# Two transformer blocks on one core: where the normalized activations h lie in SBUF, from the second norm on

## The chip, the core and the metric

The kernel runs on one core of a Trainium2 chip. The metric is the device time of one execution in microseconds (us); nanoseconds (ns) are used for single instructions. Lower is better. The kernel before took 881.18 us (median of three runs, 878.16 to 882.48). The engines are called as the profile calls them: PE is TensorE's matmul, PEld its weight load, DVE is VectorE, ACT is ScalarE, POOL is GpSimd and SP is SyncE, whose queue issues the loads.

## The reference, cut to what matters

256 tokens of width 1024 pass two blocks of a network; another 256 context tokens enter the first block's mixer. All data is float32. In short:

```python
# block 1
h   = modulate(rmsnorm(x), shift1, scale1)            # first norm; the same for the context
x  += gate1 * hgrn2_mixer(h_ctx, h, w_in[1024, 5120], w_out)
h   = modulate(rmsnorm(x), shift2, scale2)            # second norm
x  += gate2 * (silu(conv(h @ Wg)) * conv(h @ Wv)) @ w_down     # d_ff = 2816
x   = rmsnorm(x)
# block 2
h   = rmsnorm(x)                                       # third norm
p   = h @ w_in_2                                       # retention and window attention, gates
x  += rmsnorm((sig(ga) * (ret @ w_ro) + sig(gs) * (swa @ w_so)) @ w_o2)
h   = rmsnorm(x)                                       # fourth norm
x  += rmsnorm(relu(h @ w_up_2)**2 @ w_down_2)          # d_ff = 4096
```

Nearly all of the arithmetic is in the products with weights of 1024 or more rows.

## The kernel before, in words

**Three matmuls for one.** A float32 operand is split into a rounded part and a rest, both in the type fp32r. A product is then three matmuls: rounded times rounded, rounded times rest, rest times rounded. For weights, ACT writes the rounded part (tile `hi`, line 155) from the loaded tile `raw`, and DVE writes the rest (tile `lo`, line 156). For the normalized activations the two parts are `hTh` and `hTl` (lines 357 and 358): 128 partitions, 8 blocks of 1024 features over 128 partitions, 512 columns. In the first block's mixer the columns are 256 context tokens and 256 tokens; from the second norm on columns 0 to 255 are the tokens, and columns 256 to 511 hold the output of the retention later.

**Two ways to multiply with h.** A matmul has a stationary operand, 128 columns that a weight load (LDWEIGHTS) puts into the array, and a moving operand, 256 or 512 columns that stream through it. In the profile's form `out<-moving,stationary` they can be told apart.
- `fm_product` (lines 377 to 390) with `mm3` (lines 349 to 354): weights are stationary, h moves, 256 columns. One chunk of weights makes 2 x 8 x 3 = 48 matmuls. Rows `x<-hTh,hi`, `x<-hTl,hi`, `x<-hTh,lo` and the same with `m<-`.
- `mm3_rows` (lines 335 to 347), used right after a norm: h is stationary, 128 tokens at a time, and the weights move. Rows `x<-hi,hTh` and so on, 256 columns wide after the second and the fourth norm, 512 wide after the third. The mixer's `v_half` (line 756) does the same through `mm3`.

`row_product` (line 895) is the second product of each pair: activations (`ah`, `al`, or `yh`, `yl`) are stationary and weights move, 512 columns: rows `m<-hi,ah`. It reads no h.

**Order.** The program is written out in the order in which each engine executes it. PE works through: the modulation and the first two projections (to 60 us), the mixer's projections with the scan's small matmuls between (to 264 us), its output product, the second norm with the first three chunks of the up projection as `mm3_rows` (288 to 308 us), then the feed-forward part, in which two `fm_product` of 48 matmuls and one `row_product` of 24 alternate (to 475 us); the third norm with the v projection as `mm3_rows` (478 to 502 us), block 2's projections as `fm_product` with the attention's small matmuls put between them by `tick` (to 605 us), the gates and the two output products (to 686 us), the fourth norm with `mm3_rows` (688 to 702 us), and the last feed-forward part, in which one `fm_product` and one `row_product` alternate (to 869 us). Loads run on SP's queue, ahead of use, as buffers come free; `pump` (line 116) issues loads and splits.

**Where the tiles lie.** The pools are laid out one behind the other in the order of the code, and a tile has the same byte offset in all 128 partitions. In the built program of the kernel before:

```
raw buffers  18944 ..  (8 of 4096 bytes)          0 mod 512
oTs          51712                                0
hTh          59904   (16384 bytes)                0
hTl          76288   (16384 bytes)                0
x0, x1, vr   92672 ..                             0
main hi, lo  110016 ..  (5 + 5 of 4096 bytes)   448
later pools  behind them: the first stage's and the mixer's output's buffers 192,
             the buffers of all later stages (hi, lo, ah, al, swh, swl) 448
```

Every slice of h that a matmul reads starts at a multiple of 512 bytes from `hTh` or `hTl`, and every slice of weights at a multiple of 512 bytes from its buffer, so the place modulo 512 is that of the tile. In this text the **offset** of a matmul is the place of its moving operand less the place of the stationary operand that is loaded for the next matmul, modulo 512. In the kernel before it is 64 where h moves over weights at 448, and 448 (that is, 64 behind) where such weights move over h.

Of the kernel before, what the change touches and what calls it, by code (L numbers as in the profile page):

```python
# [10 lines left out]
F32R = mybir.dt.float32r  # L11
# [6 lines left out]
KT = 8  # L18
# [33 lines left out]
def kernel(ctx: ExitStack, tc: tile.TileContext, a, out):  # L52
# [5 lines left out]
    res = ctx.enter_context(tc.tile_pool(name="res", bufs=1))  # L58
# [4 lines left out]
    def bank(tag):  # L63
        return ps.tile([128, 512], F32, tag=tag, name=tag, bufs=4)
# [102 lines left out]
    def use(i, keep=None, ahead=None):  # L167

        assert i == at_["u"], (i, at_["u"])
        at_["u"] += 1  # L170
        at_["rel"] = chunks[i if keep is None else keep][0]
        a0, a1 = chunks[i]
        pump(len(halves) if ahead is None else a1 + ahead)
        assert at_["s"] >= a1
        w = []
        for j in range(a0, a1):
            r = ready.pop(j)
            for k in range(halves[j][1] if r else 0):
                w.append((r[0][:, k, :], None if r[1] is None else r[1][:, k, :]))
        return w  # L180
# [5 lines left out]
    def part_done(i):  # L186

        at_["rel"] = max(at_["rel"], chunks[i][0] + 1)
        pump(len(halves))
# [159 lines left out]
    def mm3(o, w, x, start, stop):  # L349
        wh, wl = w  # L350
        xh, xl = x
        t_.matmul(o, wh, xh, start=start, stop=False)  # L352
        t_.matmul(o, wh, xl, start=False, stop=False)  # L353
        t_.matmul(o, wl, xh, start=False, stop=stop)  # L354

    oTs = res.tile([128, 4, 512], F32, name="oTs")
    hTh = res.tile([128, KT, 512], F32R, name="hTh")
    hTl = res.tile([128, KT, 512], F32R, name="hTl")

    def hT(k, c0, c1):  # L360
        return hTh[:, k, c0:c1], hTl[:, k, c0:c1]
# [170 lines left out]
    for i in range(2):  # L532
        t = res.tile([128, D], F32, name=f"x{i}")
# [174 lines left out]
    for p in range(4):  # L708
# [9 lines left out]
        else:  # L718
            for d in range(2):
                i = C["ff" if d == 0 else "fb", p]  # L720
# [174 lines left out]
    def row_product(name, n, lhs, done):  # L895

        acc = []

        def mms(j, w, kk, tok, half):
            c = slice(half * 512, half * 512 + 512)
            mm3(acc[2 * tok + half], lhs(j, kk, tok), (w[kk][0][:, c], w[kk][1][:, c]),
                j == 0 and kk == 0, j == n - 1 and kk == 1)

        def go(j):
            if not acc:
                acc.extend(bank("m") for _ in range(4))
            w = use(C[name, j])
            for kk in range(2):  # L910
                for tok in range(2):
                    for half in range(2):
                        mms(j, w, kk, tok, half)
                if kk == 0:
                    part_done(C[name, j])

        def finish(*limits):
            tail = range(n - SKEW, n)
            w = {}
            for j in tail:  # L920
                w[j] = use(C[name, j], keep=C[name, n - SKEW])
                for kk in range(2):
                    for half in range(2):
                        mms(j, w[j], kk, 0, half)
            d0, d1 = done(0, acc[0:2]), done(1, acc[2:4])
            f0 = [next(d0) for _ in range(4)][-1]
            for j in tail:
                for kk in range(2):
                    mms(j, w[j], kk, 1, 0)
            next(d1)  # L930
            for j in tail:
                if f0 and j == n - 1:
                    f0()
                    pump(limits[0])
                for kk in range(2):
                    mms(j, w[j], kk, 1, 1)
                    at_["rel"] = chunks[C[name, j]][0] + kk + 1
            for limit in limits[1:]:
                pump(limit, True)
            for _ in limits[1:]:  # L940
                next(d1)
                if held:
                    held.pop(0)()
            while held:
                held.pop(0)()
            return [x for x in d1][-1]
        return go, finish
# [8 lines left out]
    def act_lhs(store):  # L956
        def f(j, kk, tok):
            h_, l_ = store[j]
            c = slice(kk * 256 + tok * 128, kk * 256 + tok * 128 + 128)
            return h_[:, c], l_[:, c]  # L960
        return f

    def to_hT(pool, n, tok, A, B=None, tag="hf"):


        c = slice(tok * 128, tok * 128 + 128)
        z, hf = [], []
        for kq in range(2):
            z.append(bank("x"))
            for i in range(4):  # L970
                k = 4 * kq + i
                t_.transpose(z[kq][:, i * 128:(i + 1) * 128], n[:, k * 128:(k + 1) * 128], ident)
            hf.append(pool.tile([128, 512], F32, tag=tag, name="hf", bufs=2).rearrange("p (k t) -> p k t", k=4))
        z0 = z[0].rearrange("p (k t) -> p k t", k=4)

        def per_k(v):
            return v[:, 0:4].rearrange("p (k o) -> p k o", o=1).to_broadcast([128, 4, 128])

        for i in range(4):
            k = 4 + i  # L980
            zi = z[1][:, i * 128:(i + 1) * 128]
            if B is None:
                s_.activation(hf[1][:, i, :], zi, AF.Identity, scale=A[:, k:k + 1])
            else:
                s_.activation(hf[1][:, i, :], zi, AF.Identity, scale=A[:, k:k + 1], bias=B[:, k:k + 1])
        s_.activation(hTh[:, 4:8, c], hf[1], AF.Copy)
        v_.tensor_tensor(hf[0], z0, per_k(A), op=OP.mult)
        if B is not None:
            v_.tensor_tensor(hf[0], hf[0], per_k(B), op=OP.add)
        v_.tensor_copy(hTh[:, 0:4, c], hf[0])  # L990
        for kq in range(2):
            o = slice(4 * kq, 4 * kq + 4)
            v_.tensor_tensor(hTl[:, o, c], hf[kq], hTh[:, o, c].bitcast(F32), op=OP.subtract)
# [11 lines left out]
    def o1_done(tok, acc):  # L1005
# [10 lines left out]
        scaled(y, x, r)  # L1016
        yield lambda: to_hT(ok, y, tok, AB2[:, 0, :], AB2[:, 1, :])

    go, finish = row_product("o1", 4, act_lhs(ys), o1_done)
    for p in range(4 - SKEW):  # L1020
        go(p)
# [144 lines left out]
    for tok in range(2):  # L1166
        for j in range(2):
# [5 lines left out]
            def done(k):  # L1173
                if tok and k % 2:
                    at_["rel"] = chunks[C["vr", j, 0]][0] + k // 2 + 1
                    pump(len(halves))
# [324 lines left out]
```

## Time and profile before

| | |
|---|---|
| runs before, median (lowest, highest) | 881.18 us (878.16, 882.48) |
| the profiled execution's own time | 877.26 us |
| its span, first to last instruction | 875.5 us |
| mean granted clock of PE | 0.997 |
| PE busy, share of the span | 859.9 us, 98% |
| PEld, DVE, ACT busy | 780.3, 599.5, 497.7 us |
| HBM read | 159.93 MB |

Matmuls overlap: the profile gives each a duration that includes its way through the array, 0.28 us for 256 columns, while the next one starts after about 0.12 us. The pace is therefore read from start to start, in the list in order of time: the difference of two start times over the number of matmuls between them. "Busy" alone does not show it.

### The profile page before, as it was taken

The page shows a single profiled execution, that of the slowest core. Times are in us where ns is not written, and L with a number is a line of the kernel's source. Part 1 is how long each engine was busy: PE and PEld are TensorE (multiplying, and loading weights), DVE is VectorE, ACT ScalarE, POOL GpSimd, SP SyncE. Part 2 cuts the span into 40 slices and gives each one's busy share as a digit, 9 for nine tenths or more (in the row PEclk, how much of TensorE's full clock was granted, in tenths as well). Part 3 has the DMA queues.
Part 4 walks back from the last instruction along what each step waited for, and adds up shares of the span by engine and source line. Part 5 has one row for each costly group of instructions (what it writes and reads, how often), then busy time and mean ns, then how long its engine had stood idle before and what let it go on. Part 6 is the DMA issues. An engine that isn't in the chain of part 4 may idle for free.

```text
span 875.5 us, 15429 instructions
## 1 busy us (share of the span) xinstructions
PE 859.9 (98%) x6216; PEld 780.3 (89%) x6216; DVE 599.5 (68%) x935; ACT 497.7 (57%) x807; POOL 16.3 (2%) x27
## 2 busy tenths in 40 slices
PE   8999999999999999999999999999999999999997
PEld 7688898989988999999997799999999899999995
DVE  5577969776878688877768646765495687555532
ACT  4587474855856667555555646666553665444421
POOL 0000000000000000000000000000000100000000
PEclk9999999999999999999999999999999999999999
DMA  9892654825437368776753573545786097655401
GB/s 352 274 346 101 181 181 128 281 74 173 141 122 256 107 219 275 259 235 215 261 171 73 181 206 107 157 130 155 205 302 205 3 314 247 189 188 187 150 1 49
DMA packets 116360, 161.99 MB, mean 185 GB/s; under 512 B 13888, under 2 KB 95808, under 8 KB 116288
## 3 DMA queue, kind: packets, MB, share of 16 engines
q1 hardware_dynamic: 113984, 155.80, 55.6%
q10 hardware_dynamic: 2304, 5.20, 1.7%
q8 instruction: 49, 0.80, 0.4%
q14 instruction: 23, 0.19, 0.1%
HBM read 159.93 MB, written 1.05 MB: 184 GB/s over the span
## 4 chain that ended last, share of the span: by engine, by line
PE 89%; DVE 5%; ACT 3%; DMA 1%; issue 1%; POOL 0%; SPq 0%; POOLq 0%; DVEq 0%; ACTq 0%
PE m L352 17%; PE m L354 17%; PE m L353 17%; PE x L352 8%; PE x L354 8%; PE x L353 8%; PE x L685 1%; DVE lo L156 1%; PE m L342 1%; PE x L342 1%; PE m L343 1%; PE m L338 1%; DMA raw<-in_f0w_dram 1%; PE x L343 1%; PE x L338 1%
## 5 line engine op out<-in xcount | busy, mean ns | idle before, releaser
L156 DVE TENSOR_TENSOR lo<-raw,hi 128x1024 fp32r<-128x1024 f32 (+1 forms) x248 | 291.0, 1203 | 130.7 <-ACT hi L155 130.6
L155 ACT ACTIVATE hi<-raw 128x1024 fp32r<-128x1024 f32 (+1 forms) x248 | 249.6, 1039 | 117.6 <-PE x L353 50.7
L352 PE MATMUL m<-hTh,hi 128*128 128x256 f32 (+1 forms) x560 | 178.8, 319 | 1.5 <-ACT hTh L422 1.5
L353 PE MATMUL m<-hTl,hi 128*128 128x256 f32 (+1 forms) x560 | 171.0, 305 | 0.5 <-DVE hTl L429 0.5
L354 PE MATMUL m<-hTh,lo 128*128 128x256 f32 (+1 forms) x560 | 171.3, 306 | 0.1
L352 PE MATMUL x<-hTh,hi 128*128 128x256 f32 x592 | 166.0, 280 | 0.0
L354 PE MATMUL x<-hTh,lo 128*128 128x256 f32 x592 | 164.9, 279 | 0.0
L353 PE MATMUL x<-hTl,hi 128*128 128x256 f32 x592 | 164.8, 278 | 0.0
L352 PEld LDWEIGHTS m<-hTh,hi 128*128 128x128 f32 x560 | 105.7, 189 | 12.3 <-issue 5.1
L352 PEld LDWEIGHTS x<-hTh,hi 128*128 128x128 f32 x592 | 111.1, 188 | 1.0 <-ACT hi L155 0.2
L353 PEld LDWEIGHTS x<-hTl,hi 128*128 128x128 f32 x592 | 110.8, 187 | 1.0 <-issue 0.2
L354 PEld LDWEIGHTS x<-hTh,lo 128*128 128x128 f32 x592 | 111.3, 188 | 0.0
L353 PEld LDWEIGHTS m<-hTl,hi 128*128 128x128 f32 x560 | 105.8, 189 | 6.0 <-DVE hTl L429 1.1
L354 PEld LDWEIGHTS m<-hTh,lo 128*128 128x128 f32 x560 | 105.3, 188 | 5.8 <-DVE lo L156 0.3
L352 PE MATMUL m<-hi,ah 128*128 128x512 f32 x248 | 97.3, 392 | 0.0
L354 PE MATMUL m<-hi,al 128*128 128x512 f32 x248 | 96.8, 390 | 0.0
L353 PE MATMUL m<-lo,ah 128*128 128x512 f32 x248 | 96.5, 389 | 0.0
L354 PEld LDWEIGHTS m<-hi,al 128*128 128x128 f32 x248 | 46.5, 188 | 10.6 <-DVE al L1142 0.4
L353 PEld LDWEIGHTS m<-lo,ah 128*128 128x128 f32 x248 | 46.6, 188 | 8.9
L352 PEld LDWEIGHTS m<-hi,ah 128*128 128x128 f32 x248 | 46.6, 188 | 8.9 <-ACT ah L1138 0.2
L576 DVE SCALAR_TENSOR_TENSOR vr<-raw,cs,vr 128x1024 f32<-128x1024 f32 x28 | 35.9, 1281 | 0.4
L352 PE MATMUL m<-hi,hTh 128*128 128x256 f32 x128 | 35.8, 280 | 0.0
(302 smaller groups left out, 1251.5 us busy)
## 6 DMA issues: line engine op xcount, KB each, us to landing
raw<-in_ffn_w_up_dram SPq DMA_DIRECT2D x44, 512.0 KB, 5.6
raw<-in_w_in_dram SPq DMA_DIRECT2D x42, 512.0 KB, 4.1
raw<-in_hg_w_in_dram SPq DMA_DIRECT2D x36, 512.0 KB, 5.3
raw<-in_w_ada_dram SPq DMA_DIRECT2D x32, 512.0 KB, 5.5
raw<-in_w_up_dram SPq DMA_DIRECT2D x32, 512.0 KB, 4.9
raw<-in_w_down_dram SPq DMA_DIRECT2D x32, 512.0 KB, 3.6
raw<-in_ffn_w_down_dram SPq DMA_DIRECT2D x22, 512.0 KB, 4.5
raw<-in_ada_dram SPq DMA_DIRECT2D x16, 512.0 KB, 6.5
```

What stands on the lines that cost most here:

```text
L155: s_.activation(h[:, :w], r[:, :w], AF.Copy)
L156: held.append(lambda r=r, h=h, l=l, w=w: v_.tensor_tensor(l[:, :w], r[:, :w], h[:, :w].bitcast(F32), op=OP.subtract))
L338: t_.matmul(o, hTl[:, k, c], w[k][0], start=False, stop=k == KT - 1)
L342: t_.matmul(o, hTh[:, k, c], w[k][0], start=k == 0, stop=False)
L343: t_.matmul(o, hTh[:, k, c], w[k][1], start=False, stop=False)
L352: t_.matmul(o, wh, xh, start=start, stop=False)
L353: t_.matmul(o, wh, xl, start=False, stop=False)
L354: t_.matmul(o, wl, xh, start=False, stop=stop)
L576: v_.scalar_tensor_tensor(acc, w[kk][0], cs[:, k:k + 1], acc, op0=OP.mult, op1=OP.add)
L685: t_.matmul(z[:, b * 128:(b + 1) * 128], l, r, start=i == 0, stop=i == len(terms) - 1)
```

## The change

One tile of 2 x 8 x 512 + 32 elements (32,896 bytes a partition) takes the place of `hTh` and `hTl`. Up to the mixer's end the two parts are views of it from element 32 on, that is from byte 128 on; from `hTh, hTl = h_at(0)` on, ahead of the mixer's output product, they are views from element 0 on. The functions that read or write h (`hT`, `mm3_rows`, `to_hT`, `re_t`) take the names from the enclosing function, so they follow. Everything that is allocated after h moves up by 128 bytes; what is allocated before it (`raw`, `oTs`, `ident`, `ones`, `vecs`) stays.

```diff
     oTs = res.tile([128, 4, 512], F32, name="oTs")
-    hTh = res.tile([128, KT, 512], F32R, name="hTh")
-    hTl = res.tile([128, KT, 512], F32R, name="hTl")
+
+
+    h_mem = res.tile([128, 2 * KT * 512 + 32], F32R, name="hT")
+
+    def h_at(o):
+        return [h_mem[:, i:i + KT * 512].rearrange("p (k t) -> p k t", k=KT) for i in (o, o + KT * 512)]
+
+    hTh, hTl = h_at(32)
 
     def hT(k, c0, c1):
         return hTh[:, k, c0:c1], hTl[:, k, c0:c1]
@@ -1016,6 +1022,7 @@
         scaled(y, x, r)
         yield lambda: to_hT(ok, y, tok, AB2[:, 0, :], AB2[:, 1, :])
 
+    hTh, hTl = h_at(0)
     go, finish = row_product("o1", 4, act_lhs(ys), o1_done)
```

## Rows read from the trace of the kernel before

**Rows 1.** The page's part 1: busy us, share of the span, instructions, by engine.
```profile
PE 859.9 (98%) x6216; PEld 780.3 (89%) x6216; DVE 599.5 (68%) x935; ACT 497.7 (57%) x807; POOL 16.3 (2%) x27
```
**Rows 2.** The page's part 4: the chain of work that ended last, by engine.
```profile
PE 89%; DVE 5%; ACT 3%; DMA 1%; issue 1%; POOL 0%; SPq 0%; POOLq 0%; DVEq 0%; ACTq 0%
```
**Rows 3.** Windows: stretch, length, busy us of PE, PEld, DVE, ACT, POOL, clock, DMA.
```profile
329.90:447.20 117.30, 117.30 (x841) 110.51 (x840) 95.68 (x132) 68.86 (x92) 0.00 (x0) 1.00 0.73 240
502.40:605.60 103.20, 103.20 (x847) 98.79 (x846) 62.04 (x118) 61.76 (x130) 2.79 (x4) 1.00 0.52 152
719.10:868.80 149.70, 149.70 (x936) 135.25 (x935) 77.94 (x81) 64.52 (x79) 0.54 (x1) 1.00 0.47 148
```
**Rows 4.** PE in order of time: start us, us; two feed-forward products from 329.91.
```profile
329.91 0.28 PE L352 MATMUL x<-hTh,hi 128*128 128x256 f32 x1
...
341.22 0.40 PE L352 MATMUL m<-hi,ah 128*128 128x512 f32 x1
```
**Rows 5.** PE in order of time, three feed-forward products behind transposes.
```profile
308.24 0.28 PE L353 MATMUL x<-hTl,hi 128*128 128x256 f32 x1
...
324.45 0.39 PE L352 MATMUL m<-hi,ah 128*128 128x512 f32 x1
```
**Rows 6.** Groups by line and form in windows 329.9 to 447.2 and 605.5 to 637.
```profile
L352 PE MATMUL x<-hTh,hi 128*128 128x256 f32 x224 | 62.7, 280 | 0.0
...
L352 PE MATMUL m<-hTh,hi 128*128 128x256 f32 x76 | 21.1, 277 | 0.0
```
**Rows 7.** PE in order of time, block 2's projections, and the last feed-forward product.
```profile
540.81 0.28 PE L353 MATMUL m<-hTl,hi 128*128 128x256 f32 x1
...
541.99 0.28 PE L354 MATMUL m<-hTh,lo 128*128 128x256 f32 x1
...
847.13 0.28 PE L354 MATMUL x<-hTh,lo 128*128 128x256 f32 x1
```
**Rows 8.** PE in order of time, the mixer's v_half: weights move, h is stationary.
```profile
60.13 0.29 PE L352 MATMUL m<-hi,hTh 128*128 128x256 f32 x1
60.25 0.28 PE L353 MATMUL m<-lo,hTh 128*128 128x256 f32 x1
60.37 0.28 PE L354 MATMUL m<-hi,hTl 128*128 128x256 f32 x1
60.48 0.28 PE L352 MATMUL m<-hi,hTh 128*128 128x256 f32 x1
...
71.02 0.39 PE L352 MATMUL m<-hTh,hi 128*128 128x512 f32 x1
```
**Rows 9.** PE in order of time, mm3_rows after the second and the fourth norm.
```profile
300.57 0.28 PE L342 MATMUL x<-hi,hTh 128*128 128x256 f32 x1
...
304.57 0.28 PE L342 MATMUL x<-hi,hTh 128*128 128x256 f32 x1
...
697.33 0.28 PE L342 MATMUL x<-hi,hTh 128*128 128x256 f32 x1
```
**Rows 10.** PE in order of time, swh over weights, both at 448.
```profile
637.09 0.28 PE L353 MATMUL x<-swl,hi 128*128 128x256 f32 x1
...
639.85 0.28 PE L352 MATMUL x<-hTh,hi 128*128 128x256 f32 x1
```
**Rows 11.** PE in order of time, 512 columns wide, three pairs of operands.
```profile
84.53 0.39 PE L354 MATMUL m<-hTh,lo 128*128 128x512 f32 x1
...
329.69 0.39 PE L354 MATMUL m<-hi,al 128*128 128x512 f32 x1
...
478.35 0.40 PE L342 MATMUL m<-hi,hTh 128*128 128x512 f32 x1
...
479.28 0.40 PE L338 MATMUL m<-hi,hTl 128*128 128x512 f32 x1
```
**Rows 12.** Groups by line in windows 265 to 300 and 329 to 447: DVE's split.
```profile
L156 DVE TENSOR_TENSOR lo<-raw,hi 128x1024 fp32r<-128x1024 f32 x12 | 14.0, 1220 | 1.8 <-ACT hi L155 1.8
...
L156 DVE TENSOR_TENSOR lo<-raw,hi 128x1024 fp32r<-128x1024 f32 x46 | 54.2, 1219 | 9.1 <-ACT hi L155 9.1
```

## The prediction

> **What bounds the kernel now.** I read the page's engine shares first: PE is busy 98% of the span, DVE 68%, ACT 57% [rows 1]. The chain of waits then says that PE alone carries 89% of the path to the end [rows 2]. Windows over the stages that read the moved h say the same: in the first feed-forward part, in block 2's projections and in the last feed-forward part PE has no idle time at all, while DVE stands at 82%, 60% and 52% and ACT at 59%, 60% and 43% [rows 3]. So there the time is the number of matmuls times their pace, start to start. The list in order of time gives that pace, and it is not one number:
>
> - From 329.91 to 341.22 us 96 matmuls of 256 columns read h over weights: 11.31 us / 96 = 117.8 ns each [rows 4]. The reader is to see that nothing but the pace is between them: no gap, no wait.
> - From 308.24 to 324.45 us 143 of the same matmuls, at the same offset of 64: 16.21 / 143 = 113.4 ns [rows 5].
> - The 24 products with `swh`, at offset 0: 637.09 to 639.85 us are 23 steps, 120.0 ns each [rows 10].
>
> So there are paces of 113.4, 117.8 and 120.0 ns for one instruction form at one granted clock, 1.00, the 2.4 GHz level [rows 3]. The groups by line show it too: a mean of 280 ns where the pace is slow, 277 where it is fast [rows 6]. The slow pace is steady, not a sum of single stalls, and the stretch after a `row_product` always has it. What remains to find is whether the offset decides it.
>
> From the second norm on, fm_product has 56 chunks x 48 = 2688 matmuls in which h moves. By their start distances in the trace 2040 are slow (115 to 121 ns; the first at 329.91 [rows 4], the last at 847.13 [rows 7]): 672 in the first feed-forward part, 637 and 142 in block 2's projections and output products, 589 in the last part. In the projections the small matmuls of the attention cut them into runs of 12 to 48, and these are slow too: 540.81 to 541.99 us are 10 steps of 118 ns [rows 7]. 604 are fast; 44 stand at the start of a run. At 117.8 less 113.4 ns these 2040 hold 2040 x 4.4 = 9.0 us. That is all that this change can win in them.
>
> **The change part by part.** *The places.* The new tile is 128 bytes longer than the two were, so the weights go from 448 to 576 = 64 mod 512. Up to the mixer's output product h starts at byte 128 of the tile: offset 128 - 64 = 64 as before. From then on h is at 0: offset -64 = 448 where h moves, and 64 where weights move over h. `swh`, `ah` and `al` move together with the weights: 0 as before.
>
> *h moves at offset 448.* No row has this. The nearest has the roles exchanged: `v_half`, weights at 448 moving over h at 0. It is entered at the slow pace, pays 120, 120 and 110 ns (with the list's rounding to 10 ns) and then runs at (71.02 - 60.48) us / 93 = 113.3 ns to its end [rows 8]. In the trace this is the habit of offset 448: seven stretches of v_half and two of `mm3_rows` after the fourth norm, nine in all, turn fast within some five matmuls (the first at 60.48 us [rows 8], the last at 697.33 [rows 9]), whereas at 64 a stretch that starts at 118 ns stays there. Against it stands one stretch: 300.57 to 304.57 us, weights at 448 over h, 34 steps of 117.6 ns that do not turn [rows 9]; they lie among matmuls whose weights are at 192. Bounds: all fast and at once, -9.0 us; all at the pace of offset 0, 120.0 ns: 2040 x 2.2 + 604 x 6.6 = +4.5 + 4.0 = +8.5 us. I take the nearest row, v_half: all turn fast, and each of some 60 stretches that start at 118 ns today pays for its turn about (120 - 113) + (118 - 113) = 12 ns, 0.7 us in all: -8.3 us.
>
> *Weights move over h at 64 (256 columns).* After the fourth norm 96 such matmuls, nearly all fast today, may take the slow pace that offset 64 has after a disturbance: 96 x 4.4 = +0.4 us; after the second norm some 40 of 144 that are at 113 ns today, +0.2 us; bounds 0 and +0.6. I take +0.6.
>
> *512 columns.* The v projection's 96 matmuls go from offset 448 to 64. Today 478.35 to 479.28 us is 4 steps of 232 ns [rows 11]. At offset 64 the mixer's 512-wide run from 71.02 [rows 8] to 84.53 us [rows 11] has 59 steps of 229.0 ns. 96 x -3 = -0.3 us; bounds -0.4 (at the 228 ns of row_product, 23 steps from 324.45 [rows 5] to 329.69 [rows 11]) and 0.
>
> *row_product, swh.* Both operands move by 128: nothing. *Splits.* ACT and DVE read `raw`, which stays, and write weights, which move. A window with buffers at 192 among them and one with buffers at 448 alone give 1220 and 1219 ns for DVE's [rows 12]: nothing to either side. What covers it is DVE's idle time, 18% or more in each stage [rows 3]; with PE 3.8% faster in the first feed-forward products DVE goes from 82% to some 84%.
>
> *Waits and instructions.* None is added: the same instructions in the same order on every queue. The first write to h at 0 has to wait for the last read at 32 elements further on, by PE in the mixer; the output product, 96 matmuls of some 228 ns, 22 us, lies between, and PE does its work in order. Were that cover gone, ACT's copy into `hTh` would be the one to wait, with the splits of the next weights queued behind it.
>
> Sum: -8.3 + 0.6 - 0.3 = -8.0 us. On the profiled execution's own 877.3 us (the span's 875.5 and 1.8 around it) that is 869.3. This execution was faster than all three runs; I put the difference on their median: 881.2 - 8.0 = 873.2 us.
>
> The Trainium skill would have it otherwise. "TensorE: Matmul & The Clock Gate", section "Step-by-step: what each phase is for", says that PE has two independent read ports into SBUF, so that loading the next weights takes no read bandwidth from the running matmul; "SBUF — State Buffer", section "Who interferes with whom", says that PE never waits on anyone. By that rule an operand's place can't matter and the time stays 881.2. The trace does not agree as far as it goes: three paces of one form at one clock [rows 4, 5, 10], the slowest where both operands lie at the same place. Its case is within the first rival below.
>
> **The rivals.** *The pace hangs on how a run begins, not on the offset.* For it: both paces occur at offset 64 [rows 4, 5], and 34 slow matmuls at 448 [rows 9]. Against it: nine stretches at 448 turned fast by themselves, none at 64 did. Then nothing changes: 881.2 + 0.3 = 881.5 us; the same if the placement failed to follow, as when a reader of h kept the old view.
>
> *Only some entries turn.* Behind a row_product the first matmul of h comes without any gap, its weights long loaded, and no run at 448 has that entry. If those 1261 (672 + 589) stay slow, the gain is 779 x 4.4 = 3.4 us: 877.8. If it is the 779 of block 2, with their short runs, it is 5.5 us: 875.7.
>
> *Slower: the weight load meets the moving operand all the way.* At offset 0 each matmul takes 120.0 ns and none recovers [rows 10], and at 512 columns offset 448 is the worst of the three, 232 ns against 229 and 228 [rows 5, 8, 11]. If h moving 64 behind the weights catches them up in each matmul, all 2688 pay the 120.0 ns: +8.5 us, 889.7. It decides from the point where the mean of the moved matmuls exceeds today's, (2040 x 117.8 + 604 x 113.4) / 2644 = 116.8 ns. Against it: v_half runs at 113.3 with the same distance.
>
> **How the numbers follow.** Fast nearly everywhere, 0.56: 871 to 875.5. Some entries only, 0.18: 875.5 to 879, of which I count 0.12 as over 0.5%. Nothing, 0.16: 879 to 884. Slower, 0.10: 884 to 890, of which 0.02 lies within the bound. 0.5% of 881 is 4.4 us, about what the three runs' own spread of 4.3 us lets one tell. Faster: 0.56 + 0.12 = 0.68; same: 0.06 + 0.16 + 0.02 = 0.24; slower 0.08. The range 870 to 883 leaves out the slower case and little else; the likeliest case alone has 871 to 875.5.
>
> **What would show it.** Right: the stretch of 96 after a row_product in the first feed-forward part takes 96 x 113.4 = 10.9 us instead of 11.31; the group `x<-hTh,hi` falls from 280 to 277 ns or less; the stretches to 264 us, `swh` and row_product keep their paces. Wrong: 117.8 ns behind row_product, or 120. I would also be wrong if PE gets idle time in the first feed-forward part, because DVE or the loads can't follow.

## The result, and the profile after

The changed kernel takes 875.48 us (median of 8 runs, 873.56 to 876.86), the one before, run beside it, 881.26 us (8 runs, 878.16 to 882.48). The ratio is 0.9941 with a 95% interval of 0.9927 to 0.9955, which is 5.2 us (4.0 to 6.4) less; the medians lie 5.8 us apart. The profiled execution took 873.8 us with a span of 872.0, against 877.26 and 875.5 before; so 3.5 us lie between the two traces, and these are what the traces can explain.

PE is still the bound (page's part 1, busy us, share, instructions; compare [rows 1]): the same 6216 matmuls, 3.1 us less busy.

```profile
PE 856.8 (98%) x6216; PEld 778.4 (89%) x6216; DVE 599.5 (69%) x935; ACT 497.8 (57%) x807; POOL 16.3 (2%) x27
```

The windows that answer to [rows 3] (columns as there). The first and the last stretch are the two feed-forward parts, and they are as long as before for the same work: 117.2 us for 841 matmuls against 117.3, 149.5 for 937 against 149.7 for 936. Only block 2's projections have become shorter, 847 matmuls in 100.8 us against 103.2.

```profile
329.60:446.80 117.20, 117.20 (x841) 110.65 (x841) 95.70 (x132) 68.92 (x92) 0.00 (x0) 1.00 0.73 240
501.70:602.50 100.80, 100.80 (x847) 96.41 (x846) 61.93 (x118) 61.64 (x130) 2.79 (x4) 1.00 0.53 156
...
716.10:865.60 149.50, 149.50 (x937) 135.23 (x935) 77.75 (x80) 64.40 (x78) 0.54 (x1) 1.00 0.46 148
```

PE in order of time (start us, us, instruction), one fence for all that answers to [rows 4, 5, 7, 8, 9, 10, 11]. Both parts of h carry the tile name `hT` now, and lines behind 364 have moved down by six or seven.

```profile
59.83 0.29 PE L352 MATMUL m<-hi,hT 128*128 128x256 f32 x1
...
60.18 0.28 PE L352 MATMUL m<-hi,hT 128*128 128x256 f32 x1
...
70.72 0.39 PE L352 MATMUL m<-hT,hi 128*128 128x512 f32 x1
...
300.55 0.28 PE L342 MATMUL x<-hi,hT 128*128 128x256 f32 x1
...
304.55 0.28 PE L338 MATMUL x<-hi,hT 128*128 128x256 f32 x1
...
308.10 0.28 PE L354 MATMUL x<-hT,lo 128*128 128x256 f32 x1
...
324.20 0.39 PE L352 MATMUL m<-hi,ah 128*128 128x512 f32 x1
...
329.65 0.28 PE L352 MATMUL x<-hT,hi 128*128 128x256 f32 x1
...
340.96 0.39 PE L352 MATMUL m<-hi,ah 128*128 128x512 f32 x1
...
479.81 0.39 PE L342 MATMUL m<-hi,hT 128*128 128x512 f32 x1
...
482.33 0.85 PE L338 MATMUL m<-hi,hT 128*128 128x512 f32 x3
...
540.36 0.49 PE L1267 MATMUL x<-ident,sp 128*128 128x128 f32 x3
540.60 0.37 PE L352 MATMUL m<-hT,hi 128*128 128x256 f32 x1
540.81 0.28 PE L353 MATMUL m<-hT,hi 128*128 128x256 f32 x1
...
542.40 0.28 PE L352 MATMUL m<-hT,hi 128*128 128x256 f32 x1
...
634.11 0.27 PE L353 MATMUL x<-swl,hi 128*128 128x256 f32 x1
...
636.85 0.29 PE L352 MATMUL x<-hT,hi 128*128 128x256 f32 x1
...
716.13 0.28 PE L352 MATMUL x<-hT,hi 128*128 128x256 f32 x1
...
721.78 0.39 PE L352 MATMUL m<-hi,ah 128*128 128x512 f32 x1
```

What to read in it:
- v_half, whose places didn't change against each other, still turns: (70.72 - 60.18) / 93 = 113.3 ns [rows 8].
- The stretch behind a row_product did **not** turn: 329.65 to 340.96 is 11.31 us for 96 matmuls, 117.8 ns, to the hundredth what [rows 4] has at offset 64. All seven such stretches of the first feed-forward part and the 48 of each up product of the last one (716.13 to 721.78: 117.7 ns) are so. The group that was to fall from 280 to 277 ns [rows 6] has 281 in the window 329.6 to 447:

```profile
L352 PE MATMUL x<-hT,hi 128*128 128x256 f32 x224 | 62.9, 281 | 0.0
```

- The 142 behind the transposes run at 16.10 / 142 = 113.4 ns as before [rows 5].
- In block 2 a stretch behind three transposes starts with 210 ns and then takes (542.40 - 540.81) / 14 = 113.6 ns; there [rows 7] has 118.
- swh is where it was, 2.74 us / 23 = 119.1 ns with its entry [rows 10]; the 512-wide v projection takes 2.52 / 11 = 229.1 ns instead of 232 [rows 11]; mm3_rows after the second norm 4.00 / 34 = 117.6 [rows 9].

To add it up I counted over the whole list how many matmuls with h moving take 113 to 114 ns to the next start of their kind ("at 113") and how many 115 to 121 ("at 118"), and took each stage's length, from its first matmul to the next stage's:

| stage | before: us, at 113 / 118 | after: us, at 113 / 118 | difference |
|---|---|---|---|
| modulation, first projections (to 48.18 us before) | 47.07 | 46.74 | -0.33 |
| from there to the end of the mixer's output product | 240.16 | 240.15 | -0.01 |
| rows after the second norm | 19.71 | 19.78 | +0.07 |
| first feed-forward part | 169.74, 236 / 665 | 169.62, 141 / 760 | -0.12 |
| v projection, 512 wide | 24.59 | 24.38 | -0.21 |
| block 2's projections | 134.61, 285 / 616 | 132.21, 835 / 54 | -2.40 |
| gates, output products | 51.22, 0 / 142 | 50.75, 90 / 53 | -0.47 |
| rows after the fourth norm | 13.45 | 13.61 | +0.16 |
| last feed-forward part | 167.19, 80 / 575 | 166.99, 16 / 637 | -0.20 |

The sum is -3.5 us. The first row is code that the change doesn't touch; its length differs by some 2 us between the traces of this text.

### The profile page after: what moved, and what is told of

Read it like the earlier page. It is cut to its first block, busy times and chain, and to the rows that moved or that the text cites. A ratio compares the mean times of both kernels' runs of the same rounds, so it can differ in the third digit from the quotient of the medians.

```text
span 872.0 us, 15429 instructions
## 1 busy us (share of the span) xinstructions
PE 856.8 (98%) x6216; PEld 778.4 (89%) x6216; DVE 599.5 (69%) x935; ACT 497.8 (57%) x807; POOL 16.3 (2%) x27
## 4 chain that ended last, share of the span: by engine, by line
PE 89%; DVE 5%; ACT 3%; DMA 1%; issue 1%; POOL 0%; SPq 0%; POOLq 0%; DVEq 0%; ACTq 0%
PE m L352 17%; PE m L353 17%; PE m L354 17%; PE x L352 8%; PE x L353 8%; PE x L354 8%; PE x L691 1%; DVE lo L156 1%; PE m L342 1%; PE x L342 1%; PE m L343 1%; PE m L338 1%; PE x L343 1%; PE x L338 1%; DMA raw<-in_f0w_dram 1%
## 5 line engine op out<-in xcount | busy, mean ns | idle before, releaser
L352 PE MATMUL m<-hT,hi 128*128 128x256 f32 (+1 forms) x560 | 178.2, 318 | 1.4 <-ACT hT L428 1.4
L353 PE MATMUL m<-hT,hi 128*128 128x256 f32 (+1 forms) x560 | 170.5, 304 | 0.5 <-DVE hT L435 0.5
L354 PE MATMUL m<-hT,lo 128*128 128x256 f32 (+1 forms) x560 | 170.8, 305 | 0.1
L352 PE MATMUL x<-hT,hi 128*128 128x256 f32 x592 | 166.5, 281 | 0.0
L353 PE MATMUL x<-hT,hi 128*128 128x256 f32 x592 | 165.9, 280 | 0.0
L354 PE MATMUL x<-hT,lo 128*128 128x256 f32 x592 | 165.9, 280 | 0.0
L352 PEld LDWEIGHTS m<-hT,hi 128*128 128x128 f32 x560 | 105.6, 189 | 12.2 <-issue 5.1
L354 PEld LDWEIGHTS x<-hT,lo 128*128 128x128 f32 x592 | 113.0, 191 | 0.0
L352 PEld LDWEIGHTS x<-hT,hi 128*128 128x128 f32 x592 | 111.4, 188 | 1.0 <-ACT hi L155 0.2
L353 PEld LDWEIGHTS x<-hT,hi 128*128 128x128 f32 x592 | 111.1, 188 | 1.0 <-issue 0.2
L353 PEld LDWEIGHTS m<-hT,hi 128*128 128x128 f32 x560 | 105.7, 189 | 5.9 <-DVE hT L435 1.1
L354 PEld LDWEIGHTS m<-hT,lo 128*128 128x128 f32 x560 | 105.4, 188 | 5.8 <-DVE lo L156 0.3
L352 PE MATMUL m<-hi,hT 128*128 128x256 f32 x128 | 35.8, 280 | 0.0
```

## The experiments

Theory after the result: offset 448 (h 64 bytes behind the next weights) lets a stretch run at 113, at offset 64 the smaller part does (601 of some 2600 such matmuls in the trace of before); but at 448 the way in decides whether a stretch gets there, and the way in behind a row_product does not. Rivals: it is the absolute place or the one piece of memory, not the offset; the feed-forward stretches can't run at 113 at all.

**One piece of memory, old offset.** All behind h moves by 512 bytes, h stays at 0: offset 64 throughout.

```diff
-    h_mem = res.tile([128, 2 * KT * 512 + 32], F32R, name="hT")
+    h_mem = res.tile([128, 2 * KT * 512 + 128], F32R, name="hT")
...
-    hTh, hTl = h_at(32)
+    hTh, hTl = h_at(0)
```

> The one tile has 512 spare bytes instead of 128 and h stays at its start all the time, so weights lie at 448 and h at 0 as in the kernel before: offset 64 everywhere, only everything behind h is 512 bytes higher. If the offset modulo 512 is what counts: the paces of the kernel before, 117.8 ns behind every row_product and in most of block 2's short stretches, about 881 us. If it is the one piece of memory or the absolute places that brought the gain: about 875.5 us, with 113.3 ns in block 2's projections.

880.81 us (10 runs) beside 879.38 for the kernel before: ratio 1.0012 (0.9996 to 1.0028). The first feed-forward part has 236 at 113 and 665 at 118, the numbers of before; block 2's projections 10 and 890. A stretch there:

```profile
541.93 0.28 PE L353 MATMUL m<-hT,hi 128*128 128x256 f32 x1
...
543.11 0.28 PE L354 MATMUL m<-hT,lo 128*128 128x256 f32 x1
```

1.18 us / 10 = 118 ns, as in [rows 7]. Neither the one piece nor the absolute place of h does it.

**Offset 448 in the mixer too.**

```diff
-    hTh, hTl = h_at(32)
+    hTh, hTl = h_at(0)
```

> The changed kernel, but h at offset 448 from the start, in the mixer too. If the offset decides by way of the entry: the mixer's 256-wide stretches with h moving (some 300 matmuls at 117.8 ns now) turn to 113.3 ns, -1.3 us; its 288 matmuls of 512 columns with h moving go from 229 to 233 ns, +1.2 us; v_half, weights moving over h, goes from 448 to 64 and stays at 117.8 ns where it enters so, up to 384 x 4.4 = +1.7 us. About 875.5 to 878 us. If the pace hangs on the stretch alone and not on the offset: no stretch of the mixer changes, 875.5 us.

876.46 us beside 879.38: 0.9965 (0.995 to 0.9979). The mixer becomes 1.5 us longer, 218.59 us against 217.05. Its 512-wide runs are one reason: from here

```profile
71.03 0.40 PE L354 MATMUL m<-hT,lo 128*128 128x512 f32 x1
...
84.33 0.39 PE L354 MATMUL m<-hT,lo 128*128 128x512 f32 x1
```

57 steps take 13.30 us, 233.3 ns each, where the 59 of [rows 8, 11] take 229.0; for 288 matmuls that is 1.2 us. v_half, which is now at 64 and has 276 of its matmuls at 118, costs about as much, and some 130 more matmuls of 256 columns with h moving that run at 113 give back 0.6 us. So 448 suits 256 columns with h moving and costs elsewhere: by these traces, leaving the mixer at 64 was right.

**Offset 0 from the second norm on.** 512 spare bytes; h at 0 first, then 448 bytes on.

```diff
-    hTh, hTl = h_at(0)      # ahead of the mixer's output product
+    hTh, hTl = h_at(112)
```

> 512 spare bytes, weights at 448 as before, h at 448 too from the second norm on: offset 0. If the offset decides the pace: 120.0 ns in all 2688 matmuls with h moving and in the 240 of 256 columns with weights moving over h, whatever the entry, the v projection's 96 at 227 ns instead of 233: some +8.5 + 1 - 0.6, 890 us. If it does not: 881 us with both 113.3 and 117.8 ns.

886.6 us beside 879.38: 1.0071 (1.005 to 1.0091), the predicted sign at a little less than the predicted size. The first stretch behind a row_product:

```profile
331.32 0.28 PE L352 MATMUL x<-hT,hi 128*128 128x256 f32 x1
...
342.83 0.40 PE L352 MATMUL m<-hi,ah 128*128 128x512 f32 x1
```

11.51 / 96 = 119.9 ns, and no stretch leaves this pace. The 512-wide v projection is at its best here, 227.7 ns.

**Other offsets.** Three kernels, one run each, with a different place of h in each of three stages: 128, 192, 32 (second, third, fourth norm on); 96, 160, 224; 48, 480, 16. They differ from the last one only in `h_at`, which is called at all three norms (with 16, 32, 120; 8, 24, 40; 124, 104, 116).

> 512 spare bytes, weights at 448, and another offset after each norm: 128 from the second, 192 from the third, 32 from the fourth. If only the offset modulo 256 counts, 192 in block 2's projections gives what 448 gave, 113.3 ns after at most some five matmuls in nearly every stretch. 128 and 32 have no row: behind a row_product 113.3, 117.8 or 120 ns. If the entry behind a row_product alone makes the pace there, both keep 117.8 ns.

> 512 spare bytes, weights at 448; offset 96 from the second norm, 160 from the third, 224 from the fourth, no cut. If the offset counts modulo 128 (0 and 128 both gave 120.0 ns): 96 and 224 the same pace behind a row_product, 160 that of 32, 117.0 ns. If it counts modulo 256 or 512, all three may differ.

> As the one before with offset 48 from the second norm, 480 from the third, 16 from the fourth. If the pace falls steadily with the distance from offset 0 (120.0, at 32 117.0): 16 some 118.5, 48 some 115 to 117; 480, which is 32 behind, gives 117.0 or, if behind is better than ahead, 113.3 ns. If only steps of 64 count: 16 and 48 have 120.0 or 117.8.

880.67, 884.25 and 880.91 us. From the first of them:

```profile
332.82 0.28 PE L352 MATMUL x<-hT,hi 128*128 128x256 f32 x1
...
344.34 0.39 PE L352 MATMUL m<-hi,ah 128*128 128x512 f32 x1
...
544.77 0.28 PE L352 MATMUL m<-hT,hi 128*128 128x256 f32 x1
...
545.67 0.28 PE L354 MATMUL m<-hT,lo 128*128 128x256 f32 x1
```

Offset 128 takes 11.52 / 96 = 120.0 ns, like 0. Offset 192 in block 2 has stretches at 113 (here 0.90 / 8), 317 matmuls against 575 at 118. The rest never comes to 113: 96 has 120.1 ns in the mean, 160 some 119, 224 118.5, 48 118.5, 480 118.4 to 120.8, 16 118.9, 32 117.0. So of the twelve offsets seen, most of them in one stage of one execution, a steady 113 occurs at 64, 192 and 448 alone; 0 and 128 stay at 120. None of the simple rules in the expectations comes out: modulo 128 would make 96 and 224 alike, modulo 256 would have nearly all of block 2 at 113 with 192, and a pace that falls steadily with the distance from 0 would put 48 well below 16.

**The way in behind row_product, at 448.** In the changed kernel the last 512-column matmul of each chunk of a row_product is issued as two of 256 with the same stationary operand (23 in all).

```diff
+        if cut:
+            t_.matmul(o, wh, xh, start=start, stop=False)
+            t_.matmul(o, wh, xl, start=False, stop=False)
+            for c in (slice(0, 256), slice(256, 512)):
+                t_.matmul(o[:, c], wl, xh[:, c], start=False, stop=stop)
+            return
...
-                        mms(j, w, kk, tok, half)
+                        mms(j, w, kk, tok, half, kk and tok and half)
```

> The changed kernel, with the last matmul of each row_product chunk (512 columns) issued as two of 256 columns with the same stationary operand. The stretch with h moving then begins behind a matmul of 256 columns at offset 0 (120 ns), as it does behind swh, where it turned to 113.3 ns in the changed kernel. If the entry decides what happens at offset 448: 113.3 ns after some five matmuls behind every row_product, some 1300 x 4.4 = 5.7 us less, 0.3 us for the 20 cuts: 870 us. If it is what else runs beside the feed-forward parts (splits, loads) that holds 117.8 ns there: unchanged, 875.5 to 876 us.

```profile
330.47 0.40 PE L356 MATMUL m<-hi,al 128*128 128x256 f32 x2
330.70 0.29 PE L358 MATMUL x<-hT,hi 128*128 128x256 f32 x1
330.83 0.28 PE L359 MATMUL x<-hT,hi 128*128 128x256 f32 x1
330.95 0.28 PE L360 MATMUL x<-hT,lo 128*128 128x256 f32 x1
331.06 0.28 PE L358 MATMUL x<-hT,hi 128*128 128x256 f32 x1
...
341.60 0.39 PE L358 MATMUL m<-hi,ah 128*128 128x512 f32 x1
```

870.54 us beside 879.7: 0.9894 (0.9873 to 0.9914), the best version here. The stretch pays 130 and 120 ns at its start and then runs at (341.60 - 331.06) / 93 = 113.3 ns. The first feed-forward part has 874 at 113 and 19 at 118 and takes 166.79 us instead of 169.62; the last 535 and 108, 164.96 us instead of 166.99.

**The same cut at offset 64**, `h_at(32)` kept to the end.

> The same cut with h at offset 64 throughout, as before the change. If offset 64 holds the 117.8 ns whatever the entry: 117.8 ns behind every row_product, 881 us. If the entry alone decides: 113.3 ns there, some 875 us.

```profile
330.55 0.28 PE L358 MATMUL x<-hT,hi 128*128 128x256 f32 x1
...
341.86 0.40 PE L358 MATMUL m<-hi,ah 128*128 128x512 f32 x1
```

879.66 us, one run: nothing gained. 11.31 / 96 = 117.8 ns; not one of the first feed-forward part's matmuls is at 113, 897 are at 118. The cut alone is worth nothing in this run; offset and way in are needed together. Here the weights lie where the changed kernel has them, at 64 modulo 512, and block 2's projections take 135.77 us: the weights' new place by itself does nothing either.

**Offset 448 in block 2 only.** `h_at(32)` at the second norm, `h_at(0)` at the third, `h_at(32)` at the fourth.

> The changed kernel with offset 64 kept in both feed-forward parts; only block 2's projections and output products have 448. If the change's gain comes from their short stretches alone, as the trace of the changed kernel reads (some 920 of 1100 matmuls at 113.3 ns, the feed-forward parts at 117.8 ns with either offset): the time of the changed kernel, 875 to 877 us. If the feed-forward parts gave part of it after all: 877 to 881 us.

876.25 us beside 880.17: 0.9959 (0.9944 to 0.9974). Block 2's projections take 132.22 us (816 at 113, 74 at 118), the changed kernel's 132.21; the feed-forward parts 170.52 and 167.52 us with 901 and 644 at 118. A stretch of block 2:

```profile
541.60 0.28 PE L354 MATMUL m<-hT,lo 128*128 128x256 f32 x1
...
543.53 0.28 PE L353 MATMUL m<-hT,hi 128*128 128x256 f32 x1
```

1.93 us / 17 = 113.5 ns. So most of the change's gain is block 2's.

**A break at the other end.** In the changed kernel, row_product whole; of the fm_product behind it the second matmul is issued as two of 128 columns.

```diff
...
+                    t_.matmul(zi, wk_[0], xk[0], start=True, stop=False)
+                    for h in (slice(0, 128), slice(128, 256)):
+                        t_.matmul(zi[:, h], wk_[0], xk[1][:, h], start=False, stop=False)
+                    t_.matmul(zi, wk_[1], xk[0], start=False, stop=False)
...
```

> The changed kernel, h at 448; row_product is left whole, but the second matmul of the fm_product behind it is issued as two of 128 columns with the same stationary operand. If any break in the rhythm lets a stretch at offset 448 turn: 113.3 ns behind every row_product, -5.7 us and some 0.1 us for each of 25 cuts: 871 to 873 us. If it has to be the matmul of 256 columns at offset 0 that comes before: 117.8 ns remains, 876 to 878 us.

```profile
332.35 0.28 PE L396 MATMUL x<-hT,hi 128*128 128x256 f32 x1
332.46 0.34 PE L398 MATMUL x<-hT,hi 128*128 128x128 f32 x2
332.64 0.33 PE L399 MATMUL x<-hT,lo 128*128 128x256 f32 x1
...
333.17 0.28 PE L352 MATMUL x<-hT,hi 128*128 128x256 f32 x1
...
343.37 0.39 PE L352 MATMUL m<-hi,ah 128*128 128x512 f32 x1
```

873.07 us beside 880.17: 0.9914 (0.99 to 0.9929). The two halves take 180 ns, some 60 more than one matmul, and behind them the stretch runs at (343.37 - 333.17) / 90 = 113.3 ns; all seven stretches behind a row_product do, and the 13 of the later stages. But two of the 22 breaks don't stand behind a row_product's matmul, and both stretches stay at 117.8 ns: the one from 449 us, which has this pace in the changed kernel's trace too, and the first 141, behind transposes, which are at 113 there without a break. So a break can be of another kind and at another place, and row_product itself isn't what holds the pace; but a break doesn't turn every stretch at 448.

## Why the prediction was nearly right, step by step

The time came out at 875.5 where 873.2 was predicted, by a smaller gain. That it is so near is in part luck: the prediction's own sign of being wrong, "117.8 ns behind row_product", is what the trace shows. The traces' 3.5 us are the size of the second rival's gain, 3.4 us, and not of the 8.0 that were added up. The medians lie about halfway between, and only a part of what they moved beyond the traces is explained below.

- **h moving, all stretches turn, -8.3 us: this step failed in its "all".** It was taken from v_half, which is entered from matmuls of 256 columns, and no row had the entry behind row_product at 448. Those stretches stayed at 117.8 ns [rows 4 against the fence above], as the second rival said ("Only some entries turn"), with 3.4 us for 779 x 4.4. Measured: block 2's projections 550 more at 113, x 4.4 = 2.4 us, the stage's -2.40; the output products 90, 0.4 us, -0.47. In the feed-forward parts 95 and 64 went the other way, +0.7 us.
- **row_product, "nothing".** Not quite: its 625 matmuls behind such stretches took 228.1 and 227.9 ns in the mean before and 227.1 and 226.8 after, some 0.65 us less. That offsets the 0.7 us, so that the feed-forward parts are not longer in spite of these 95 and 64 matmuls. It goes with the offset of the stretch ahead: in the kernel with 448 in block 2 only they are at 228.1 and 227.9 again.
- **Weights moving over h at 64, +0.6:** +0.07 and +0.16 us. After the fourth norm 47 are at 113 and 45 at 118 where it was 85 and 5; after the second, 4 are at 113 where it was 40, and the stage is hardly longer.
- **v projection, -0.3:** 233.6 to 229.4 ns in the mean, the stage -0.21, as predicted but for the size.
- **Splits, waits: nothing.** DVE's busy time is 599.5 us in both; PE has no idle time in the three windows.

The medians moved by more than the traces do, 5.8 us against 3.5. 1.2 of the 2.3 can be named: the trace of before has 275 matmuls of block 2 (605.6 to 637 us, the last line of [rows 6]) at 113, and in the two other traces with offset 64 there that stage takes 135.79 and 135.77 us instead of 134.61. So the trace of before was a lucky one: which pace a stretch takes differs between executions of the same offsets. The rest lies in executions without a trace and stays open.

By the rule of the Trainium skill ("TensorE: Matmul & The Clock Gate", "Step-by-step: what each phase is for") that a weight load takes no read bandwidth from the running matmul, place could not matter. The measurements decide against it here: the same instructions in the same order take 886.6 us with h at offset 0 and 880.81 with h at 64.

What stays open is what in a way in decides. A first distance of 200 to 210 ns mostly leads to 113 in block 2, but the same entry behind transposes went to 118 for 71 matmuls in the kernel with the cut row_product:

```profile
699.90 0.36 PE L358 MATMUL x<-hT,hi 128*128 128x256 f32 x1
700.10 0.28 PE L359 MATMUL x<-hT,hi 128*128 128x256 f32 x1
...
702.22 0.28 PE L359 MATMUL x<-hT,hi 128*128 128x256 f32 x1
```

(2.12 us / 18 = 117.8 ns). The weight loads give a hint. Three groups of them: a stretch at 113.3 ns (before, 606 to 636 us), a slow one at 448 (the changed kernel, 330 to 340.8 us), one in the kernel with offset 0 (332 to 342.7 us).

```profile
L354 PEld LDWEIGHTS m<-hTh,lo 128*128 128x128 f32 x75 | 14.1, 188 | 0.0
...
L354 PEld LDWEIGHTS x<-hT,lo 128*128 128x128 f32 x31 | 6.0, 192 | 0.0
...
L354 PEld LDWEIGHTS x<-hT,lo 128*128 128x128 f32 x30 | 5.8, 192 | 0.0
```

At 113.3 ns every load takes 187 or 188 ns; at 120.0 every load takes 192; in the slow stretch at 448 every third one does, the one shown. In a slow stretch at 64 (before, 330.2 to 341 us) all have 187 or 188, too. That loads and moving reads meet in the memory would fit the longer loads and the dependence on the two places, but the slow pace at 64 shows nothing of it in the loads, and no run shows the cause.

## What to carry to other kernels

Where PE is never idle, read its pace from start to start before anything else: one form at one clock had paces of 113.3, 117.8 and 120.0 ns here, 6% apart, and the time was only that. If there are several, try the moving operand at other places against the next stationary one, in each stage by itself, and take no stage's habit for another's: the gain predicted for the feed-forward parts came only when a single matmul ahead of each stretch, or the second one in it, was cut in two. A price should be taken from a row that has the same entry, and where there is none, the entry is the uncertain term.

## What was not expected of the hardware

- With the same clock, offset and instructions a stretch stays at 113.3 or at 117.8 ns for up to 275 matmuls, and one cut matmul ahead of it moves it from one to the other at offset 448 (875.5 to 870.5 us), not at 64 (879.66, one run).
- The best offset for 256 columns is not the best for 512: 512-wide matmuls took 226.8 to 228.1 ns at 0, 229.0 to 229.4 at 64 and 233.3 to 233.6 at 448, while at 256 columns offset 0 has the slowest pace, 120.0 ns.
- Where weights move over h at 64 behind the output product o2, half of them run at 113 from the start (47 of 94 in the changed kernel's trace); the prediction priced all 96 at the slow pace.
